# Binding the eight 64-column products of a pair of heads into one uninterrupted run on TensorE

## The chip, the cores and the metric

The kernel runs on one core of a Trainium2 chip. The metric is the device time of one execution in microseconds; the median of several runs is compared. Engines are called PE or TensorE (matrix products), PEld (its weight loads), DVE or VectorE, ACT or ScalarE, POOL or GpSimd, and SP (which issues most transfers).

## The reference, cut to what matters

The program is an encoder trunk of two layers on 512 tokens of 1024 features: feed-forward, token mixer, attention into a memory of 256 tokens, feed-forward, each followed by a layer norm. The change lies in the mixer of the first ("even") layer:

```python
def mixer_ab(h, w_in, w_out, q_gain, k_gain, sink, ang_2d, ang_1d):
    qa, ka, va, qb, kb, vb = jnp.split(h @ w_in, AB_SPLITS, axis=-1)
    ...                                   # per-head RMS norm of qa, ka; rotary of all q, k
    out_a = global_gqa(qa, ka, va)        # 8 query heads of 64, 2 key heads: every token sees every token
    out_b = window_gqa_sink(qb, kb, vb, sink)   # 8 heads: only tokens within +-128, a sink logit per head
    return jnp.concatenate([out_a, out_b], axis=-1) @ w_out

# for one head, in both halves:
    s = einsum('qd,sd->qs', q, k) * 64 ** -0.5
    p = softmax(s)
    o = einsum('qs,sd->qd', p, v)         # the product that the change concerns
```

## The kernel before

All 512 tokens stay on the chip. A matrix product of full precision is made of three products of rounded parts (`mm3`), in 512-column banks of PSUM; a bank is named by its tag: `a` (3 banks), `d` (2) and `t` (3). Sixteen heads are worked off in order, eight global ones (`weights_a`) and eight windowed ones (`weights_b`), two to a pair: pair `pr`, half `s`. For one head the steps are:

- `scores`: for each of four blocks of 128 queries two products into a bank `a` (512 columns; 256 or 384 for windowed heads).
- The minimum on VectorE, the exponential and the normalisation on ScalarE (`softmax`), into a tile `t2`.
- `turned`: for each block `kk` of 128 keys, TensorE transposes the weights into a bank `t` and a copy brings them to a `slab` tile; three copies run on VectorE, the one for `kk == 3` on ScalarE.
- `attend`, once for a pair: eight products into one bank `d`. Each multiplies 64 columns of values by the turned weights. The first head (`s == 0`) writes partitions 0 to 63 of the bank, the second 64 to 127, and the loop takes the heads alternately: block 0 of head 0, block 0 of head 1, block 1 of head 0, and so on. Both operands are plain float32, so that the profile has two records for each of these products ("128*64" in its rows; other products are "128*128").

Between the heads stands work of other kinds (`aside`): the last columns of the input projection (`last_columns`, 48 products a block into a bank `d`), the turning of the windowed values and keys, and shares of the output projection (`share`, 12 products of 512 columns into a bank `d`). After the mixer the memory stage follows, whose weights are loaded and split in two parts by ScalarE and VectorE while the mixer still runs.

None of this is the order in which instructions are issued. `Graph.record` writes every operation down with its dependences and a cost, so that all of them carry one line number in the profile (L159). `Graph.plan` then simulates the five engines with these costs and gives each engine a fixed order: whenever an engine is free, it takes the ready operation with the lowest key, the key being the place in the recorded program (`rank`), and for VectorE, ScalarE and GpSimd, in a second pass, the latest start that keeps TensorE on time (`deadlines`). If the product with the lowest key is not ready, another one goes first. For a product with 64 rows or columns the cost is halved (`beside` in `cost`).

Of the kernel before, what the change touches and what calls it, by code (L numbers as in the profile page):

```python
# [23 lines left out]
NT = S // P  # L24
# [41 lines left out]
class Graph:  # L66
# [3 lines left out]

    LATENCY = {"tensor": 200.0, "vector": 115.0, "scalar": 135.0, "gpsimd": 90.0, "sync": 90.0}
    PATIENT = ("vector", "scalar")
    URGENT = ("vector", "scalar", "gpsimd")
    ENGINES = ("tensor", "vector", "scalar", "gpsimd", "sync")

# [64 lines left out]
    def record(self, engine, method, args, kw):  # L140
        kw = dict(kw)
        aps = [z for z in list(args) + list(kw.values()) if hasattr(z, "tensor")]
        outs = [kw[k] for k in ("out", "accum_out") if k in kw]
        if "out" not in kw:
            outs.insert(0, args[0])
        ins = [z for z in aps if not any(z is o for o in outs)]
        op = Op()
        op.engine, op.index, op.dma, op.adds = engine, len(self.ops), method == "dma_start", "accum_op" in kw
        op.rank = op.index
        op.ns = self.cost(engine, method, outs[0], ins, kw)  # L150
        func = args[2] if method == "activation" else None
        op.table = str(func) if func in (AF.Silu, AF.Exp) else None
        op.size = math.prod(outs[0].shape) * 4
        op.thin = op.dma and engine == "sync" and op.size >= 2**19 and outs[0].shape[0] <= 64
        op.port = method in ("tensor_tensor", "scalar_tensor_tensor", "tensor_scalar") and (
            engine == "gpsimd" or engine == "vector" and math.prod(outs[0].shape[1:]) >= 64 and all(z.space != bass.MemoryType.PSUM for z in ins)
        )
        fn = getattr(getattr(self.nc, engine), method)
        op.call = lambda: fn(*args, **kw)  # L159
        op.deps, op.users, op.frees, op.later = set(), [], [], []  # L160
        if self.after and engine in self.after[1]:
            op.deps.add(self.after[0])
        for z, writes in [(z, False) for z in ins] + [(z, True) for z in outs]:
            info = self.tiles.get(z.tensor.name)
            if info is None:
                continue
            p0, p1, runs = self.extent(z)
            opens = writes and kw.get("start", False)
            keep = []
            for q, w, a0, a1, other in info["log"]:  # L170
                over = opens or p0 < a1 and a0 < p1 and (
                    info["bank"] and q.engine != engine or any(l < b and a < h for l, h in runs for a, b in other)
                )
                if over and (w or writes or info["bank"] and q.engine != engine) and q is not op:
                    op.deps.add(q)
                covered = writes and p0 <= a0 and a1 <= p1 and all(any(l <= a and b <= h for l, h in runs) for a, b in other)
                if not covered:
                    keep.append((q, w, a0, a1, other))
            keep.append((op, writes, p0, p1, runs))
            info["log"] = keep  # L180
            info["users"].add(op)
        self.ops.append(op)

    def plan(self):

# [28 lines left out]
        def arrive(e):  # L214
            while heaps[e] and heaps[e][0][0] <= now[e]:
                _, key, i, op = heapq.heappop(heaps[e])
                heapq.heappush(ready[e], (key, i, op))
# [6 lines left out]
        while len(order) < len(self.ops):  # L224
            best = None
            for e in self.ENGINES:
                arrive(e)
                if ready[e] and e in self.PATIENT:
                    key, _, op = ready[e][0]
# [72 lines left out]
    def emit(self):  # L302
# [10 lines left out]
        for op in self.ops:  # L313
            if op.engine in self.URGENT:
                op.key = last[op]
# [7 lines left out]
class Kernel:  # L323
# [683 lines left out]
    def mixer_ab(self, ln_i, last):  # L1007
        nc, a = self.nc, self.a
# [148 lines left out]
        def attend(po, pts, vp):  # L1157
            for kk in range(NT):
                for s in range(2):
                    lo, hi, pt = pts[s][kk]  # L1160
                    nc.tensor.matmul(
                        po[64 * s : 64 * s + 64, lo:hi], vp[:, kk, 64 * s : 64 * s + 64], pt, start=kk == 0, stop=kk == NT - 1,
                        skip_group_check=True,
                    )

        w2 = self.w_cols512(w_in, 1024)
        vt, vt_, qb_ = self.t2(F32), [], {}
# [42 lines left out]
        for n, (f, v, pr, s) in enumerate(heads):  # L1210
            pts = turned(us.pop(0))
            for g, _, *at in heads[n + 2 : n + 3]:
                us.append(g(*at))
            if s == 1 and n + 3 < len(heads):
                made[n >= 5, heads[n + 3][2]] = queries(qb if n >= 5 else qa, heads[n + 3][2], n >= 5)
            if s == 0:
                kept = pts
            else:
                po = self.ps("d")
                attend(po, (kept, pts), v if n < 8 else vb[0])  # L1220
                if n < 8:
                    acts.append(self.split_t2(po))
                else:

                    h, l = self.pair()
                    self.split(
                        po.rearrange("p (r c) -> p c r", r=ROWS), *(z.rearrange("p (c r) -> p c r", r=ROWS) for z in (h, l))
                    )
                    acts.append((h, l))
            for g in aside.get(n, []):  # L1230
                g()
            if n == 13:
                self.memory_tokens()
# [436 lines left out]
```

## Time and profile before

| | |
|---|---|
| median of 3 runs | 2127.72 us (2126.93 to 2129.83) |
| the profiled execution | 2127.48 us, of which the span of instructions 2125.7 us |
| granted TensorE clock | 0.998 of full speed |
| PE busy | 2109.5 us, 99% of the span |
| DVE busy | 1727.3 us, 81% |
| ACT busy | 1141.2 us, 54% |

Times in the views are counted from the start of the span. "Busy" is the time in which at least one instruction of the engine runs; products overlap their neighbours at both ends, so that the distance from one start to the next is the better price. In rows of the timeline, equal instructions that follow each other are one row with their count ("x3"), and a bracket at the end holds the idle time ahead of it and what ended that. The chain is followed back from the last instruction, from each step to what released it.

### The profile page before, as it was taken

How to read it: one execution, taken by the hardware profiler on the slowest of the kernel's cores; microseconds unless marked ns; L12 is line 12 of the kernel's file. 1: busy time of each engine (PE TensorE's matmuls, PEld its weight loads, DVE VectorE, ACT ScalarE, POOL GpSimd, SP SyncE). 2: the span in 40 equal slices, each digit the busy share in tenths (PEclk: the TensorE clock that was granted, in tenths of full speed). 3: DMA queues.
4: the chain of work that ended last, by engine and by line, in shares of the span. 5: the costliest groups of instructions: out<-in, count | busy, mean ns of one | idle time of the engine just before them, and what ended most of it. 6: DMA issues, size and time to landing. Idle time of an engine off the chain costs nothing.

```text
span 2125.7 us, 32517 instructions
## 1 busy us (share of the span) xinstructions
PE 2109.5 (99%) x12584; PEld 1850.5 (87%) x12584; DVE 1727.3 (81%) x2479; ACT 1141.2 (54%) x1855; POOL 278.4 (13%) x375
## 2 busy tenths in 40 slices
PE   9999999999999999999999999999999999999997
PEld 7999987767888899998889999888888888999996
DVE  7789988777748879998879999866578479699997
ACT  5555543687546554445445455457765465444552
POOL 0001014310002000000200000312210011000003
PEclk9999999999999999999999999999999999999999
DMA  6566562004433346664446556256454433456551
GB/s 205 142 167 148 135 189 90 21 21 119 138 121 109 90 123 175 153 156 129 149 100 147 123 138 190 73 143 168 118 164 156 139 91 98 109 149 154 144 150 60
DMA packets 208858, 275.91 MB, mean 130 GB/s; under 512 B 10688, under 2 KB 151616, under 8 KB 208704
## 3 DMA queue, kind: packets, MB, share of 16 engines
q1 hardware_dynamic: 175904, 221.14, 33.8%
q0 software_dynamic: 32512, 52.44, 14.2%
q8 instruction: 99, 1.62, 0.3%
q14 instruction: 55, 0.45, 0.1%
q10 hardware_dynamic: 288, 0.26, 0.0%
HBM read 259.12 MB, written 4.19 MB: 124 GB/s over the span
## 4 chain that ended last, share of the span: by engine, by line
PE 96%; DVE 2%; DMA 1%; ACT 1%; SPq 0%; issue 0%; DVEq 0%; POOL 0%; ACTq 0%
PE a L159 59%; PE d L159 23%; PE t L159 15%; DVE slab L159 1%; DVE x L159 1%; DMA slab<-t 1%; SPq L159 0%; ACT t L159 0%; DMA raw<-x_t 0%; ACT slab L159 0%; DVE t L159 0%; DVE xl L159 0%; ACT xh L159 0%; POOL lny L159 0%; DVEq L1666 0%
## 5 line engine op out<-in xcount | busy, mean ns | idle before, releaser
L159 DVE TENSOR_TENSOR slab<-slab,slab 128x1024 fp32r<-128x1024 f32 (+3 forms) x638 | 727.9, 1166 | 71.1 <-ACT slab L159 41.5
L159 ACT CAST slab<-slab 128x1024 fp32r<-128x1024 f32 (+2 forms) x498 | 472.4, 983 | 342.3 <-DVE slab L159 170.5
L159 PE MATMUL a<-slab,slab 128*128 128x256 f32 (+3 forms) x2320 | 566.7, 322 | 0.7 <-DMA slab<-t 0.5
L159 PE MATMUL a<-xh,slab 128*128 128x256 f32 (+2 forms) x2480 | 560.1, 315 | 0.1
L159 PEld LDWEIGHTS a<-slab,slab 128*128 128x128 f32 x2320 | 409.7, 190 | 45.6 <-ACT t L159 3.4
L159 PEld LDWEIGHTS a<-xh,slab 128*128 128x128 f32 x2480 | 416.5, 190 | 33.6 <-ACT slab L159 1.0
L159 PE MATMUL d<-slab,slab 128*128 128x512 f32 (+3 forms) x1792 | 442.5, 395 | 0.2 <-DVE x L159 0.2
L159 PE MATMUL a<-xl,slab 128*128 128x256 f32 (+1 forms) x1240 | 389.7, 314 | 0.0
L159 PE MATMUL a<-raw,slab 128*128 128x256 f32 x2048 | 389.0, 283 | 0.1
L159 PEld LDWEIGHTS d<-slab,slab 128*128 128x128 f32 (+1 forms) x1792 | 308.0, 185 | 66.8 <-issue 11.8
L159 PEld LDWEIGHTS a<-raw,slab 128*128 128x128 f32 x2048 | 327.9, 192 | 5.5 <-ACT slab L159 0.6
L159 PEld LDWEIGHTS a<-xl,slab 128*128 128x128 f32 x1240 | 236.1, 190 | 18.1
L159 PE MATMUL t<-slab,slab 128*128 128x512 f32 (+1 forms) x840 | 209.7, 389 | 1.0 <-DVE x L159 1.0
L159 DVE TENSOR_TENSOR slab<-raw,slab 128x1024 fp32r<-128x1024 f32 (+2 forms) x140 | 160.0, 1159 | 17.5 <-ACT slab L159 17.2
L159 PEld LDWEIGHTS t<-slab,slab 128*128 128x128 f32 x840 | 149.9, 189 | 27.5 <-issue 1.3
L159 ACT CAST slab<-raw 128x1024 fp32r<-128x1024 f32 (+1 forms) x132 | 124.2, 970 | 23.5 <-PE a L159 8.7
L159 DVE SCALAR_TENSOR_TENSOR x<-d,x 128x512 f32<-128x512 f32 x168 | 114.7, 685 | 23.5 <-PE d L159 22.6
L159 ACT COPY t<-a 128x512 f32<-128x512 f32 (+1 forms) x116 | 63.4, 549 | 129.9 <-PE a L159 76.7
L159 DVE TENSOR_TENSOR slab<-t,slab 128x512 fp32r<-128x512 f32 (+1 forms) x158 | 101.9, 660 | 12.8 <-ACT slab L159 12.5
L159 ACT CAST slab<-t 128x512 fp32r<-128x512 f32 (+1 forms) x158 | 90.2, 588 | 37.9 <-DVE t L159 14.4
L159 POOL DMA_DIRECT2D slab<-ffn_w_down x40 | 47.7, 1193 | 309.9 <-DVE slab L159 280.1
L159 ACT ACTIVATE t<-a 128x512 f32<-128x512 f32 (+3 forms) x65 | 36.3, 559 | 93.2 <-PE a L159 93.2
(127 smaller groups left out, 2191.3 us busy)
## 6 DMA issues: line engine op xcount, KB each, us to landing
slab<-ffn_w_gate SPq DMA_DIRECT2D x80, 512.0 KB
slab<-ffn_w_up SPq DMA_DIRECT2D x80, 512.0 KB
slab<-ffn_w_down SPq DMA_DIRECT2D x80, 512.0 KB
slab<-ffn_w_down POOLq DMA_DIRECT2D x40, 512.0 KB, 5.7
raw<-mem_w_kv SPq DMA_DIRECT2D x16, 1024.0 KB
slab<-t SPq DMA_DIRECT2D x96, 128.0 KB
slab<-ffn_w_gate POOLq DMA_DIRECT2D x16, 512.0 KB, 7.6
slab<-ffn_w_up POOLq DMA_DIRECT2D x16, 512.0 KB, 6.0
```

Source lines behind the costliest of these rows:

```text
L159: op.call = lambda: fn(*args, **kw)
```

## The change

After the eight products of a pair are recorded, `join` binds them. The first product gets the dependences of all eight, so the planner lets the run begin only when everything that it reads is there. Each of the others depends on the one before it and gets the rank -1, which makes it the first choice of TensorE as soon as its predecessor is issued. The planner's cost of the first and of the last product rises by 95 ns each. Only the planned order changes; what an instruction on the chip waits for is still its own operands.

```diff
     PATIENT = ("vector", "scalar")
+    TURN = 95.0
     URGENT = ("vector", "scalar", "gpsimd")
...
+    def join(self, n):
+
+        run = self.ops[-n:]
+        for prev, op in zip(run, run[1:]):
+            run[0].deps |= op.deps.difference(run)
+            op.deps.add(prev)
+            op.rank = -1
+        run[0].ns += self.TURN
+        run[-1].ns += self.TURN
...
                         skip_group_check=True,
                     )
+            nc.join(2 * NT)
```

The built programs hold the same instructions. Three places of TensorE's order follow. In the names, `d_725`, `d_893` and `d_942` are the banks of the first, fourth and fifth pair; `slab_556` and `slab_754` hold values of global and windowed heads; the other `slab` of a 64-row product holds turned weights; `ident` marks a transpose.

TensorE at the first pair, from its first product on, before (`slab_676`, `slab_679` are the turned weights of head 0, `slab_702`, `slab_705` those of head 1; `a_693` to `a_715` are scores of a later head):

```order
L159 MATMUL d_725_806<-slab_676_757,slab_556_637 64x512
L159 MATMUL a_693_774<-slab_600_681,slab_668_749 128x512 x2
L159 MATMUL a_707_788<-slab_602_683,slab_668_749 128x512
L159 MATMUL t_706_787<-ident_1_78,t2_653_734 128x128
L159 MATMUL t_706_787<-ident_1_78,t2_657_738 128x128
L159 MATMUL t_706_787<-ident_1_78,t2_661_742 128x128
L159 MATMUL t_706_787<-ident_1_78,t2_665_746 128x128
L159 MATMUL a_707_788<-slab_602_683,slab_668_749 128x512
L159 MATMUL a_711_792<-slab_602_683,slab_668_749 128x512 x2
L159 MATMUL d_725_806<-slab_702_783,slab_556_637 64x512
L159 MATMUL a_715_796<-slab_602_683,slab_668_749 128x512 x2
```

Two products stand alone; after the last row and four transposes come a piece of two, two scores and a piece of four. The same place now:

```order
L160 MATMUL d_725_806<-slab_676_757,slab_556_637 64x512
L160 MATMUL d_725_806<-slab_702_783,slab_556_637 64x512
L160 MATMUL d_725_806<-slab_676_757,slab_556_637 64x512
L160 MATMUL d_725_806<-slab_702_783,slab_556_637 64x512
L160 MATMUL d_725_806<-slab_679_760,slab_556_637 64x512
L160 MATMUL d_725_806<-slab_705_786,slab_556_637 64x512
L160 MATMUL d_725_806<-slab_679_760,slab_556_637 64x512
L160 MATMUL d_725_806<-slab_705_786,slab_556_637 64x512
L160 MATMUL a_719_800<-slab_602_683,slab_668_749 128x512 x2
```

The scores `a_693` to `a_715` and the transposes `t_706` moved ahead of the run, which is unbroken and takes the heads in turn.

TensorE at the fourth pair, where the windowed heads begin, before (`t_895` are the first transposes of a windowed head, `slab_850` and `slab_873` the turned weights of key blocks 2 and 3 of the two heads; two more products of this pair stand alone further up):

```order
L159 MATMUL d_893_974<-slab_870_951,slab_556_637 64x512 x2
L159 MATMUL d_893_974<-slab_850_931,slab_556_637 64x512
L159 MATMUL d_893_974<-slab_873_954,slab_556_637 64x512
L159 MATMUL d_893_974<-slab_850_931,slab_556_637 64x512
L159 MATMUL d_893_974<-slab_873_954,slab_556_637 64x512
L159 MATMUL t_895_976<-ident_1_78,t2_853_934 128x128
L159 MATMUL t_895_976<-ident_1_78,t2_857_938 128x128
```

And now (`d_917` is a share of the output projection):

```order
L160 MATMUL t_895_976<-ident_1_78,t2_853_934 128x128
L160 MATMUL d_917_998<-slab_813_894,slab_839_920 128x512
L160 MATMUL t_895_976<-ident_1_78,t2_857_938 128x128
L160 MATMUL a_887_968<-slab_845_926,slab_837_918 128x256 x2
L160 MATMUL d_917_998<-slab_812_893,slab_839_920 128x512
L160 MATMUL d_893_974<-slab_847_928,slab_556_637 64x512
L160 MATMUL d_893_974<-slab_870_951,slab_556_637 64x512
L160 MATMUL d_893_974<-slab_847_928,slab_556_637 64x512
L160 MATMUL d_893_974<-slab_870_951,slab_556_637 64x512
L160 MATMUL d_893_974<-slab_850_931,slab_556_637 64x512
L160 MATMUL d_893_974<-slab_873_954,slab_556_637 64x512
```

The transposes `t_895` now stand ahead of the fourth pair's run, and seven products of the share stand ahead of them, where three did before.

TensorE at the fifth pair, before (its first three products, two of 256 and 384 columns together and one of 384, stand a few rows further up; `t_940` turns queries, `a_936` are scores):

```order
L159 MATMUL d_942_1023<-slab_899_980,slab_754_835 64x256
L159 MATMUL d_944_1025<-slab_809_890,slab_726_807 128x512
L159 MATMUL t_923_1004<-ident_1_78,t2_884_965 128x128
L159 MATMUL t_923_1004<-ident_1_78,t2_888_969 128x128
L159 MATMUL d_942_1023<-slab_919_1000,slab_754_835 64x256
L159 MATMUL t_940_1021<-ident_1_78,slab_554_635 128x128
L159 MATMUL t_940_1021<-ident_1_78,slab_555_636 128x128 x2
L159 MATMUL t_940_1021<-ident_1_78,slab_556_637 128x128
L159 MATMUL d_942_1023<-slab_919_1000,slab_754_835 64x384
L159 MATMUL d_942_1023<-slab_922_1003,slab_754_835 64x384
L159 MATMUL a_936_1017<-slab_845_926,slab_892_973 128x256 x2
L159 MATMUL d_942_1023<-slab_922_1003,slab_754_835 64x256
```

And now:

```order
L160 MATMUL d_942_1023<-slab_896_977,slab_754_835 64x256
L160 MATMUL d_942_1023<-slab_919_1000,slab_754_835 64x256
L160 MATMUL d_942_1023<-slab_896_977,slab_754_835 64x384
L160 MATMUL d_942_1023<-slab_919_1000,slab_754_835 64x384
L160 MATMUL d_942_1023<-slab_899_980,slab_754_835 64x384
L160 MATMUL d_942_1023<-slab_922_1003,slab_754_835 64x384
L160 MATMUL d_942_1023<-slab_899_980,slab_754_835 64x256
L160 MATMUL d_942_1023<-slab_922_1003,slab_754_835 64x256
L160 MATMUL a_936_1017<-slab_845_926,slab_892_973 128x256 x2
```

Six pieces became one run; of the share `d_944`, one product stood ahead of the last piece before, and four stand ahead of the run now.

## The prediction

> **What bounds the kernel now.** I read the page's first part, then the chain that ended last, then the waits of TensorE in the mixer (390 to 560 us), to see whether time taken from TensorE there is time taken from the end.
>
> ```profile
> PE 2109.5 (99%) x12584; PEld 1850.5 (87%) x12584; DVE 1727.3 (81%) x2479; ACT 1141.2 (54%) x1855; POOL 278.4 (13%) x375
> ...
> PE 96%; DVE 2%; DMA 1%; ACT 1%; SPq 0%; issue 0%; DVEq 0%; POOL 0%; ACTq 0%
> ...
> PE d L159 <- DVE x L159: 0.2, 1, 0.2
> ```
>
> TensorE holds 96% of the chain, and the last row is the only recorded wait in those 170 us (columns: us in total, times, longest). So the end moves with TensorE's own time, until another engine becomes late. A busy TensorE is not one at its peak, though, so next I asked what the 64-column products cost. Each of the eight pairs of heads has a bank `d` of its own; this view takes TensorE's work on `d` in eight stretches, one for each pair (columns: stretch, its length, busy us and records).
>
> ```profile
> 409.50:418.23 8.73, 5.09 (x16) 1.00 0.00 0
> 431.00:436.35 5.35, 4.64 (x16) 1.00 0.00 0
> 449.20:453.68 4.48, 3.79 (x16) 1.00 0.10 24
> 458.10:468.60 10.50, 5.72 (x16) 1.00 0.09 28
> 473.90:482.66 8.76, 5.98 (x18) 1.00 0.00 0
> 493.85:496.19 2.34, 2.29 (x16) 1.00 0.05 3
> 506.20:509.50 3.30, 2.93 (x16) 1.00 0.73 278
> 517.20:521.08 3.88, 3.58 (x16) 1.00 0.19 36
> sum 47.34, PE 34.02; mean PE 4.25
> ```
>
> The work is equal in the first four (global heads, 512 columns) and equal in the last four (windowed heads, 256 or 384), and every product is two records, yet the cost goes from 3.79 to 5.72 and from 2.29 to 5.98. The timeline of the first pair tells why (start, us, then what ran; the distance to the next row is what a row really takes).
>
> ```profile
> 409.57 1.07 PE L159 MATMUL d<-slab,slab 128*64 128x512 f32 x2
> 410.57 0.96 PE L159 MATMUL a<-slab,slab 128*128 128x512 f32 x3
> ...
> 414.70 1.08 PE L159 MATMUL d<-slab,slab 128*64 128x512 f32 x4
> 415.71 0.73 PE L159 MATMUL a<-slab,slab 128*128 128x512 f32 x2
> 416.37 1.94 PE L159 MATMUL d<-slab,slab 128*64 128x512 f32 x8
> 418.24 0.72 PE L159 MATMUL d<-slab,xh 128*128 128x512 f32 x2
> ```
>
> One product alone (x2) takes 1.00 us, two products (x4) take 1.01, four take 1.87. The two heads of a pair use different halves of the array's columns and run side by side if they stand next to each other; a lone one leaves half of the array empty for a whole microsecond. A further pair in a run costs 1.87 - 1.01 = 0.86.
>
> **The change, part by part.** It adds no instruction and removes none. The built orders differ on TensorE between the transposes of the first pair and the mixer's last rows, on VectorE and ScalarE in the same stretch, and in a swap of two output transfers at the very end, of the same size and not the last to leave, which I cost at nothing. The transfers on POOL keep their order, and SP's keep theirs but for that swap; so SP's loads of weights are moved past nothing. All eight pairs stand as unbroken runs of eight, heads alternating, where before there were 22 pieces (4, 2, 2, 3, 6, 1, 2, 2 by pair).
>
> *Term 1, the products themselves.* The price of a bound run is in the trace: for windowed heads the sixth stretch, 2.29; for global heads 1.01 + 3 x 0.86 = 3.59, and the same from a piece of seven products that fills four places:
>
> ```profile
> 432.78 3.65 PE L159 MATMUL d<-slab,slab 128*64 128x512 f32 x14
> 436.36 0.73 PE L159 MATMUL d<-slab,xh 128*128 128x512 f32 x2
> ```
>
> That is 3.58. Eight runs: 4 x 3.58 + 4 x 2.29 = 23.48, against 34.02, a difference of 10.54. Two corrections: the fifth stretch holds two 128-column products of another `d` (x18), about 0.5; and the busy time of each piece runs 0.07 into the next row (409.57 + 1.07 against 410.57), which 14 pieces fewer no longer do: 1.0. Term 1 is **-9.0 us**.
>
> *Term 2, the turns.* Work between two pieces is itself slower. The third pair shows two score products squeezed between two halves, and an earlier row shows six in one go:
>
> ```profile
> 449.29 1.94 PE L159 MATMUL d<-slab,slab 128*64 128x512 f32 x8
> 451.16 0.74 PE L159 MATMUL a<-slab,slab 128*128 128x512 f32 x2
> 451.82 1.94 PE L159 MATMUL d<-slab,slab 128*64 128x512 f32 x8
> 453.69 0.66 PE L159 MATMUL t<-ident,t 128*128 128x128 f32 x4
> ...
> 406.46 1.54 PE L159 MATMUL a<-slab,slab 128*128 128x512 f32 x6
> 407.84 0.40 PE L159 MATMUL d<-slab,xl 128*128 128x512 f32 x1
> ```
>
> Two squeezed products take 451.82 - 451.16 = 0.66; at the free pace (1.38 / 6 = 0.23) they take 0.46. So a break costs 0.20 outside the pieces, beside what term 1 holds. 14 breaks go: **-2.8 us**. [...] Were the turn free, the sum would rest on term 1 alone, 2.8 us higher.
>
> *Term 3, what is late next.* A lone product used to be issued as soon as its own operand was there; now it stands behind work that was pulled ahead of it, and TensorE reaches that work sooner. What must keep up is VectorE and ScalarE. Their load from the first piece to the last, and in two stretches where the present kernel runs them hard (columns: stretch, length, then busy us of PE, PEld, DVE, ACT, POOL):
>
> ```profile
> 409.60:521.00 111.40, 111.16 (x587) 75.40 (x586) 87.93 (x243) 91.01 (x217) 10.45 (x40) 1.00 0.18 48
> 490.00:510.00 20.00, 20.00 (x121) 15.28 (x120) 18.36 (x55) 17.80 (x47) 2.25 (x8) 1.00 0.58 159
> 535.00:560.00 25.00, 25.00 (x133) 21.25 (x132) 23.80 (x38) 14.20 (x22) 2.22 (x6) 1.00 0.37 118
> ```
>
> 111.40 less 11.8 is 99.6: VectorE would be busy for 88% of it and ScalarE for 91%. The other two rows have them at 92% and 89%, and at 95% and 57%, with no wait on TensorE. So the load is bearable; queues are the danger. The tightest place that I find is the passage to the windowed heads, where the first transposes of a windowed head (`t_895`) now stand ahead of the fourth pair's run instead of behind it. Before, it reads:
>
> ```profile
> 447.16 0.60 PE L159 MATMUL t<-ident,t 128*128 128x128 f32 x4
> ...
> 468.61 0.76 PE L159 MATMUL t<-ident,t 128*128 128x128 f32 x5
> ...
> 448.27 0.58 ACT L159 COPY slab<-t 128x512 f32<-128x512 f32 x1
> ...
> 449.40 0.59 ACT L159 ACTIVATE slab<-t 64x512 fp32r<-64x512 f32 x1 [0.55 <-PE t L159]
> ...
> 453.81 0.59 ACT L159 CAST slab<-d 128x512 fp32r<-128x512 f32 x1 [1.05 <-PE d L159]
> ...
> 459.89 0.58 ACT L159 COPY slab<-t 128x512 f32<-128x512 f32 x1 [0.78 <-PE t L159]
> ...
> 464.10 0.59 ACT L159 COPY slab<-t 128x512 f32<-128x512 f32 x1 [0.83 <-PE t L159]
> ...
> 465.09 1.91 ACT L159 ACTIVATE t<-t,l 128x256 f32<-128x256 f32 x4
> ```
>
> From the transposes that feed the 448.27 copy to `t_895`, TensorE took 468.61 - 447.16 = 21.45. Now the three pieces of the fourth pair (1.00 + 1.00 + 3.58) and four breaks (0.8) leave that stretch, two score products of 256 columns follow instead of preceding (0.2), the third pair's halves shrink by 0.15, and four more products of the output share, seven for three, come in (0.9): about 15.6. ScalarE, from that copy to the normalisation at 465.09, took 16.82, of which the four idle times are 3.21: 13.6 of work. The margin was 468.61 - 465.09 - 0.50 = 3.0 and is now 15.6 - 13.6, or 2.0 less whatever idling ScalarE keeps. Should it keep all 3.2, TensorE waits 1.2. The same squeeze in the fifth pair, whose stretch loses 5.98 to 2.29 and already held the 0.2 wait, I put at 0.8. So **+2.0 us**; the ends are -1.0 (no wait at all, and the short stalls on transposes there shrink too) and +7 (the squeeze at each of six later pairs).
>
> *Inside a run* I cost waiting at nothing: the copy that comes last, of the other head's third and fourth key block, is read first by the sixth product, 5 x 0.43 = 2.1 us after a global run's start, which is the cover. If the copy is later than that, TensorE stands still with the rest of its queue.
>
> Sum: 2127.48 (the profiled execution: span 2125.7 and 1.8 around it; 0.24 below the median shown) - 9.0 - 2.8 + 2.0 = **2117.7 us**.
>
> **The rivals.** (A) *The softmax chain keeps its pace.* Scores, minimum, exponential, normalisation, transposes and copies run round over ScalarE, and what TensorE saves it waits. [...] Against: its idle times are mostly waits for TensorE (`PE t`, `PE d` in the rows above), which shrink with it. If waits take back 10 of the 11.8 us the time is 2125.7: no change. (B) *The next stage is not ready.* The memory projections start 12 us sooner, and their weights pass through VectorE:
>
> ```profile
> 553.33 1.21 DVE L159 TENSOR_TENSOR slab<-raw,slab 128x1024 fp32r<-128x1024 f32 x1
> ...
> 557.41 1.07 PE L159 MATMUL a<-slab,slab 128*128 128x512 f32 x4
> ```
>
> This half is done at 554.54 and first read within the second row, 3.2 us later. If VectorE's queue, 95% full there, did not move at all, TensorE would wait 11.8 - 3.2 = 8.6, and 2124.3 results. Against: the split stands between parts of the layer norm that are released by TensorE, and so it moves with it. (C) *Slower:* each run waits for its last copy, because ScalarE has exponentials ahead of it, and nothing else may pass. With w us for each of eight runs the gain is gone at w = 11.8 / 8 = 1.5 and the kernel is slower beyond the bound at w = 2.0; at 2.5 it takes 2135.7. Against it stands the 2.1 us of cover, so that a copy would have to be over 4 us late, eight times, where the whole stretch now has one wait. (D) *Nothing is saved:* the runs are unbroken but some of them do not overlap their halves, as in the piece at 465.03 before, where two products of one head stood together. The new order alternates throughout, so I hardly believe it.
>
> **How the numbers follow.** The forecast has 0.76, and its own range is 2127.5 - 11.8 - 1.0 = 2114.7 to 2127.5 - 11.8 + 7 = 2122.7. (A) has 0.09, (B) 0.09, (C) 0.04, (D) 0.02. About 0.2% (4.3 us) is what a measurement here can tell from no change; faster means below 2123.5. The forecast is faster wholly, of (A) and (B) together 0.05, when waits take back only part. So faster 0.81, same 0.15, slower 0.04. The range of 0.8 runs from 2114.0 to 2123.5: the likeliest case whole, and its edge of (A) and (B).
>
> **What would show it.** In the profile after, stretches of `d` should read about 3.6 and 2.3 with x16 each, their sum near 23.5 (terms 1 and 2 right); score products beside a run should keep the 0.66 only once for each side. Waits of TensorE on `a`, `t` or `d` within the mixer should add up to about 2 us; if they add up to 8 or more, (A) or (C), told apart by whether a `t`/`a` row or a `d` row waits; waits on `a` at the start of the memory stage mean (B). Rows from the memory stage on should be the old ones shifted by some 10 us. I am wrong if ScalarE's order puts copies behind exponentials that themselves wait, which no trace of the old order can show.

## The result, and the profile after

| | before | after |
|---|---|---|
| median | 2128.38 us (4 runs, one more than above) | 2115.42 us (2114.70 to 2117.81, 4 runs) |
| ratio | | 0.9941 (95% interval 0.9924 to 0.9958) |
| ratio of a second measurement (5 runs, 2115.9 us) | | 0.9947 (0.9935 to 0.9960) |
| profiled execution, span | 2127.48, 2125.7 us | 2117.81, 2116.0 us; second one: span 2113.8 us |

The kernel is faster by 0.5 to 0.6%, 12 to 13 us. The page's first part and its chain after the change:

```profile
PE 2099.0 (99%) x12584; PEld 1847.6 (87%) x12584; DVE 1725.2 (82%) x2479; ACT 1141.1 (54%) x1855; POOL 280.3 (13%) x375
...
PE 95%; DVE 2%; DMA 1%; ACT 1%; SPq 1%; issue 0%; DVEq 0%; POOL 0%; ACTq 0%
```

The counts are the old ones, and PE is busy for 10.5 us less. TensorE's work on `d` in the eight stretches, one for each pair, as it was shown of before (columns: stretch, its length, busy us and records, then granted clock and DMA; in four rows the product ahead of the run ends just inside the stretch, hence x17):

```profile
413.40:417.05 3.65, 3.57 (x16) 1.00 0.00 0
430.40:434.06 3.66, 3.57 (x16) 1.00 0.00 0
447.50:451.10 3.60, 3.58 (x16) 1.00 0.00 0
462.27:465.86 3.59, 3.59 (x17) 1.00 0.02 5
472.45:474.75 2.30, 2.30 (x17) 1.00 0.00 0
484.60:486.94 2.34, 2.29 (x16) 1.00 0.00 0
497.97:500.27 2.30, 2.30 (x17) 1.00 0.42 169
509.65:511.95 2.30, 2.30 (x17) 1.00 1.06 370
sum 23.74, PE 23.50; mean PE 2.94
```

All global pairs cost the same, all windowed ones too, and each at the price of the best unbroken run of before (3.58 and 2.30 from start to next start): 23.50 against 34.02. Where the mixer ends, at the memory stage's first key products, TensorE stands here, before and after (timelines of the two kernels; start, us, what ran):

```profile
548.10 1.19 PE L159 MATMUL a<-slab,slab 128*128 128x512 f32 x5
```

```profile
536.94 1.41 PE L160 MATMUL a<-slab,slab 128*128 128x512 f32 x6
```

The first changed instruction starts at 408.49 before and 408.91 after, so that the mixer holds nearly the whole gain and the memory stage starts without delay. For every kernel below I give the same measure: the distance from the first changed transpose to the first product behind the last changed row, 139.61 us before and 128.35 after ("the mixer"), and in it the sum of the pieces, from each piece's start to the next start ("the pieces", 32.66 and 23.55). The rest is 106.95 and 104.80.

### The profile page after: what moved, and what is told of

Same layout as the page of the kernel before. It is cut to its first block, busy times and chain, and to the rows that moved or that the text cites. A ratio compares the mean times of both kernels' runs of the same rounds, so it can differ in the third digit from the quotient of the medians.

```text
span 2116.0 us, 32513 instructions
## 1 busy us (share of the span) xinstructions
PE 2099.0 (99%) x12584; PEld 1847.6 (87%) x12584; DVE 1725.2 (82%) x2479; ACT 1141.1 (54%) x1855; POOL 280.3 (13%) x375
## 4 chain that ended last, share of the span: by engine, by line
PE 95%; DVE 2%; DMA 1%; ACT 1%; SPq 1%; issue 0%; DVEq 0%; POOL 0%; ACTq 0%
PE a L160 59%; PE d L160 22%; PE t L160 14%; DMA slab<-t 1%; DVE slab L160 1%; ACT t L160 1%; SPq L160 1%; DVE x L160 1%; DMA raw<-c_w_out 0%; DVE t L160 0%; ACT slab L160 0%; DMA raw<-x_t 0%; DVE xl L160 0%; ACT xh L160 0%; DVE mn L160 0%
## 5 line engine op out<-in xcount | busy, mean ns | idle before, releaser
L160 PE MATMUL d<-slab,slab 128*128 128x512 f32 (+4 forms) x1792 | 432.0, 394 | 0.0
```

## The experiments

| kernel | median, ratio to before (interval) | pieces | mixer |
|---|---|---|---|
| changed kernel again | 2115.90, 0.9947 (0.9935 to 0.9960) | 23.55 | 128.34 |
| bound in twos | 2119.74, 0.9960 (0.9948 to 0.9973) | 24.46 | 130.81 |
| head by head | 2128.45, 1.0002 (0.9993 to 1.0011) | 35.13 | 139.83 |
| two and two | 2117.19, 0.9951 (0.9936 to 0.9966) | 23.96 | 128.67 |
| windowed pairs only | 2122.28, 0.9976 (0.9967 to 0.9985) | 28.00 | 134.16 |
| global pairs only | 2120.90, 0.9966 (0.9953 to 0.9978) | 27.63 | 132.95 |
| no extra planner cost | 2119.62, 0.9962 (0.9949 to 0.9976) | 23.55 | 129.97 |
| larger extra planner cost | 2119.14, 0.9959 (0.9947 to 0.9972) | 23.55 | 130.57 |
| dependences not gathered | 2123.37, 0.9978 (0.9968 to 0.9987) | 27.87 | 134.29 |
| more work on ScalarE | 2119.28, 0.9958 (0.9945 to 0.9972) | 23.55 | 130.11 |

**The changed kernel again**, without an edit.

> The changed kernel once more, for a tighter ratio and a second profile. In the first profile the mixer stretch of TensorE, from the first changed transpose to the first row after the last changed one, lasts 128.35 us (139.61 before), and 2.4 us of waits for the small transfers slab<-t stand in the odd mixer (0.5 before). If these waits belong to one execution alone, this profile has the same 128.3 us in the even mixer and about 0.5 us in the odd one; if they are a lasting price of the new order, about 2.4 again. Time 2115 to 2117 us, ratio near 0.994.

The mixer is the same to 0.01 us. The waits for the small transfers `slab<-t` in the odd mixer, of before, of the first and of the second profile after (us in total, times, longest):

```profile
PE a L159 <- DMA slab<-t: 0.5, 2, 0.3
```

```profile
PE a L160 <- DMA slab<-t: 2.4, 6, 0.5
```

```profile
PE a L160 <- DMA slab<-t: 0.7, 3, 0.3
```

The same kernel shows 2.4 and 0.7, so most of the 2.4 belonged to that execution and not to the order; the first profile caught the slowest of its four runs.

**Head by head or two by two.** Is it the overlap of the two halves that pays, or the unbroken run?

```diff
-            for kk in range(NT):
-                for s in range(2):
+            for s in range(2):
+                for kk in range(NT):
```

> Eight products of a pair still bound in one run, but the four of the first head first and then the four of the second, so that neighbours use the same half of the columns. Theory 1: only the fourth and fifth product of a run can overlap; 7 places of 0.86 us instead of 4 in a global run, and the like in a windowed one: the runs add up to about 40.8 us instead of 23.55, the mixer to about 145.6, the time to about 2132.6, slower than the kernel before by 0.2%. Theory 2 (turns and the unbroken run alone): the same number of runs, so the mixer stays near 128.4 and the time near 2115.4.

The eight runs stand unbroken, and the whole gain is gone: the time is that of before (1.0002, interval 0.9993 to 1.0011). The first run (timeline; the next row's start ends it):

```profile
413.03 5.42 PE L160 MATMUL d<-slab,slab 128*64 128x512 f32 x16
418.38 0.72 PE L160 MATMUL a<-slab,slab 128*128 128x512 f32 x2
```

It takes 418.38 - 413.03 = 5.35 instead of 3.58. What lies outside the pieces keeps its gain (139.83 - 35.13 = 104.70, against 104.80 in the changed kernel and 106.95 before), so fewer breaks are worth some 2.2 us by themselves; the pieces lose 11.6 us with the overlap and are 2.5 longer than before, which eats it up. So unbroken runs paid here only because their halves overlap (3.58 us against 5.35). My size was wrong, though: seven places of 0.86 were counted and six were taken, so the pieces add up to 35.13 and not 40.8, and the kernel is no slower than before where 0.2% was expected. Why six? In the second variant the order is 0, 0, 1, 1, 0, 0, 1, 1 by heads.

```diff
-            for kk in range(NT):
-                for s in range(2):
-                    lo, hi, pt = pts[s][kk]
+            for s, kk in [(s, kk) for half in range(2) for s in range(2) for kk in (2 * half, 2 * half + 1)]:
+                for lo, hi, pt in (pts[s][kk],):
```

> The eight products of a pair bound in the order two of the first head, two of the second, two of the first, two of the second. Taking heads one by one (four and four) a global run took 5.35 us, six places of 0.86 and the turns, where I had counted seven. Theory A (TensorE starts a product of the free half up to two products, four records, ahead of its turn): two and two overlap wholly, a global run takes 3.6 us and a windowed one 2.3, the time is that of the bound kernel, 2115 to 2117. Theory B (products start in the order of the program, and the six places had another cause): five to six places, a global run takes 4.4 to 5.2 us, the eight runs 28 to 33 us, and the time is 2120 to 2125.

```profile
413.14 3.71 PE L160 MATMUL d<-slab,slab 128*64 128x512 f32 x16
416.77 0.74 PE L160 MATMUL a<-slab,slab 128*128 128x512 f32 x2
```

3.63 us: all but the 3.58 of the alternating order. Theory A's forecast of 3.6 us holds; the starts of the records stand at the end.

**Bound in twos**, so that no product is alone but work may come between.

```diff
-            nc.join(2 * NT)
+                nc.join(2)
```

> Only the two products of one key block, one of each head, are bound; other work may stand between such twos. The built order has 14 pieces (8 in the bound kernel, 22 before), and no product alone. Theory 1 (a lone product leaves half of the array empty, and beside that each break costs about 0.35 us, 0.15 of it inside the piece and 0.2 outside): the pieces add up to about 24.5 us (23.55 bound, 32.66 before), the mixer to about 130.4 us, the time to about 2117.5. Theory 2 (it is the unbroken run of eight as such that saves): 6 of the 14 saved breaks are back, so 6/14 of the 11.3 us saved are lost: mixer 133.2, time about 2120.

The first pair shows a break:

```profile
411.88 1.08 PE L160 MATMUL d<-slab,slab 128*64 128x512 f32 x4
412.89 0.73 PE L160 MATMUL a<-slab,slab 128*128 128x512 f32 x2
...
414.45 2.80 PE L160 MATMUL d<-slab,slab 128*64 128x512 f32 x12
417.17 0.50 PE L160 MATMUL d<-slab,xh 128*128 128x512 f32 x1
```

1.01 and 2.72 are 3.73 where an unbroken run takes 3.58: a break costs 0.15 inside. Six more breaks made the pieces 24.46 - 23.55 = 0.91 longer (0.15 each, as theory 1 had it), and the rest of the mixer 106.35 - 104.80 = 1.55, of which about 0.6 are short stalls that were added (records that take over 0.05 us more than others between the same neighbours) and 0.16 a break are left. The mixer, 130.8, is that of theory 1 (130.4), not of theory 2 (133.2); the median, 2119.7, is nearer to theory 2's. What it has beyond the mixer lies outside; two places there differ between executions and kernels (below), but that they make it up is not shown.

**Half of the pairs.** First the windowed ones alone, then the global ones alone.

```diff
-            nc.join(2 * NT)
+            if vp is not va:
+                nc.join(2 * NT)
```

> Only the four windowed pairs are bound; the four global ones are planned as before. The built order has 15 pieces: 11 global ones, with the same split as before the change, and 4 runs. Theory 1: the pieces add up to 28.1 us (-4.5 against before), seven breaks fewer take another 0.16 each outside (-1.1): mixer about 134.0 us, time about 2122. Rival (the gain comes from the shorter softmax chain at the passage to the windowed heads, where the fourth pair now stands behind the first windowed transposes): with the fourth pair split as before, most of the windowed gain is lost again in waits and the mixer stays above 137 us.

Pieces 28.00 (28.1 expected), mixer 134.16 (134.0), median 2122.3 (2122): theory 1 to within 0.2 us. The rival, by which the gain lies at the passage to the windowed heads, had the mixer above 137.

```diff
-            nc.join(2 * NT)
+            if vp is va:
+                nc.join(2 * NT)
```

> The complement of the windowed experiment: only the four global pairs are bound. The built order has 14 pieces: 4 runs and ten windowed pieces, split much as before the change. Theory 1 (lone products and breaks): the pieces add up to 27.7 us (-4.9 against before) and eight breaks fewer take 0.16 each outside (-1.3): mixer about 133.4 us, time about 2121.5; with the -5.44 us that binding the windowed pairs alone gave, the two halves add up to the -11.26 us of the whole change. Theory 3 (the parts help each other, by what is pulled forward): the sum of the halves falls short of the whole by 2 us or more, so that this mixer stays above 135 us.

Pieces 27.63 (27.7 expected), mixer 132.95 (133.4), median 2120.9. The halves save 5.45 and 6.66, together 12.1, where the whole change saves 11.26. Theory 3 wanted the halves to save 2 us or more less than the whole; they save 0.85 more, so it fails. Of the 0.85, 0.58 lies in the pieces: with only the global pairs bound, the windowed ones fell into ten pieces of 13.29 us, where before they were eleven of 13.87. The gain is, but for such bits, a sum over the pairs.

**How it is bound.** The run's first product no longer gets the dependences of the others:

```diff
-            run[0].deps |= op.deps.difference(run)
```

> join without the line that gives the first product the dependences of all eight: a run may begin when its first operand is there, and if a later one is not, other work is put between. The built order has 17 pieces, five of them begin with a product alone and four end with one. Theory 1: the pieces add up to 28.0 us (+4.4 against the bound kernel) and nine more breaks take 0.16 each (+1.4): mixer about 134.2 us, time about 2121.5. Rival (TensorE waits inside the runs, so that the line's worth is the waits it avoids): the pieces stay as long as in theory 1, but waits on d of 2 us or more come on top.

Pieces 27.87 (28.0 expected), mixer 134.29 (134.2). The waits of TensorE in the mixer:

```profile
PE t L160 <- ACT t L160: 0.9, 1, 0.9
PE t L160 <- DVE slab L160: 0.3, 1, 0.3
```

None is on `d`: no run waits inside; the run just falls apart, since a product whose operand is late lets other work in. The line matters for 5.9 us of the mixer, half of the gain there. The median, 2 us above the expectation, is not explained by the mixer. Then the planner's cost of the turn, 0 and 180 instead of 95:

```diff
-    TURN = 95.0
+    TURN = 0.0
```

> The runs stay bound, and the planner's extra 95 ns for the first and the last product are set to 0. Theory 1: the order has the same 8 runs (23.55 us) and the planner is 0.2 us a run more hopeful, which moves few rows: mixer within 1 us of 128.35, time within 2 us of the bound kernel. Rival (the planner's knowledge of the turn is what keeps TensorE from waiting): the mixer gets 2 us or more longer, with recorded waits on t or d.

```diff
-    TURN = 95.0
+    TURN = 180.0
```

> The bound kernel with 180 ns instead of 95 ns as the planner's extra cost of the first and the last product, since a break was measured at about 0.35 us. Theory (the planner's times only have to be roughly right): the same 8 runs, mixer within 0.7 us of 128.35, time 2115 to 2117. Rival (a truer cost lets TensorE wait less): the 1.3 us of short stalls that are left in the mixer shrink, mixer 127.3, time 2114.5.

The pieces stay, and both mixers are longer, by 1.6 and 2.2 us. Both theories missed: the first allowed 1 us and 0.7, the rival of the first wanted 2 us or more with waits on `t` or `d`, the rival of the second wanted it faster. The waits in the mixer with 180 are

```profile
PE t L160 <- DVE slab L160: 0.7, 1, 0.7
PE t L160 <- ACT t L160: 0.5, 1, 0.5
PE a L160 <- DVE mn L160: 0.3, 1, 0.3
```

and short stalls, as defined above, add up to about 3.4 us (3.0 with 0, 1.3 in the changed kernel). Neither a lower nor a truer cost helps, yet three points do not make 95 an optimum: small shifts of the planned order move the stalls by some 2 us.

**How near ScalarE is to being the limit.** Eight more copies, one for each global head:

```diff
                 self.softmax(u, P, mn, 0, S, sums=ps)
+                if t == 0:
+                    nc.scalar.activation(self.junk[:, :512], u, AF.Copy)
```

> The bound kernel with eight more copies on ScalarE, one of 128x512 for each global head, into a tile that nobody reads: some 8 x 0.7 = 5.6 us of ScalarE between 409 and 465 us, where ScalarE is busy for 51.5 of 56 us and TensorE has no recorded wait. If the idle rest of 4.5 us can be used, TensorE loses about 1 us (mixer 129.5, time 2117). If ScalarE's idle time is bound in the chain and can't be used, so that the softmax chain was already at its limit, TensorE loses nearly all of it (mixer 134, time 2121).

From 409 to 512 us, the changed kernel and this one (stretch, length, busy us of PE, PEld, DVE, ACT, POOL):

```profile
409.00:512.00 103.00, 103.00 (x605) 75.10 (x604) 89.49 (x248) 93.62 (x223) 11.24 (x41) 1.00 0.23 62
```

```profile
409.00:512.00 103.00, 102.14 (x595) 73.72 (x594) 88.96 (x247) 95.84 (x228) 11.26 (x41) 1.00 0.19 52
```

The copies took 0.64 us each, 5.1 in all, and the mixer grows by 1.76, a third of that, between the two expectations and nearer to the first. So ScalarE, at 91%, was not yet the limit. How much room is left is not shown: the copies also shift the planned order, and the two kernels above lost 1.6 and 2.2 us by such a shift alone. At 93% TensorE has holes of 0.86 us in this stretch, and the largest waits for VectorE (waits of TensorE in the mixer):

```profile
PE t L160 <- DVE slab L160: 0.7, 1, 0.7
PE a L160 <- ACT t L160: 0.2, 1, 0.2
```

## Why the prediction was right

Forecast 2117.7 us with a range of 2114.0 to 2123.5; measured 2115.4 and 2115.9. The direction and the mechanism of terms 1 and 2 hold, by the experiments and not only by the sum; term 3 does not.

- **Term 1, the products: -9.0 forecast, -9.1 measured** (32.66 to 23.55). That a lone product takes the time of two (1.00 us against 1.01 before) is what decides it: the order that keeps the runs and takes away the overlap loses all 11 us of the mixer.
- **Term 2, the turns: -2.8 forecast, -2.15 measured** for everything outside the pieces (106.95 to 104.80), what term 3 came to included; the two other orders of eight runs give 104.70 and 104.71. The order in twos gives 0.16 for a break outside the piece; I had taken 0.20 from a break with products on both sides. By the records of before, the row ahead of a piece takes 0.1 us longer; behind it a product takes 0.335 instead of 0.227 us, a transpose only 0.164 instead of 0.109, and some breaks had transposes behind them.
- **Term 3, the new waits: +2.0 forecast, about +0.1 measured.** This is the mis-sized step. No wait of TensorE is recorded in the mixer, not at the fifth pair either, and its short stalls went from about 1.2 to 1.3 us. The passage to the windowed heads, after the change:

```profile
445.34 0.66 PE L160 MATMUL t<-ident,t 128*128 128x128 f32 x4
...
461.27 0.27 PE L160 MATMUL t<-ident,t 128*128 128x128 f32 x1
...
446.08 0.57 ACT L160 COPY slab<-t 128x512 f32<-128x512 f32 x1
447.31 0.69 ACT L160 ACTIVATE t<-a,mn 128x512 f32<-128x512 f32 x1 [0.66 <-DVE mn L160]
...
451.25 0.59 ACT L160 CAST slab<-d 128x512 fp32r<-128x512 f32 x1 [0.50 <-PE d L160]
...
460.35 1.00 ACT L160 ACTIVATE t<-t,l 128x256 f32<-128x256 f32 x2
```

TensorE needs 461.27 - 445.34 = 15.93 (15.6 forecast). ScalarE idles 1.16 instead of 3.21 and is done with the first normalisation at 460.85: a margin of 0.42, where I had let it keep all its idling and had TensorE wait 1.2. All four of the old idle times waited for TensorE; 0.50 us of that is left, and 0.66 now waits for VectorE.

The margin itself was also worked out wrongly. In the 3.0 of before, the 1.11 us from the transposes to the copy (448.27 - 447.16) and the 0.50 of the first normalisation are taken off; in the new 15.6 - 13.6 = 2.0 they are not. Worked out alike it is 0.4 with no idling, and with all of it TensorE would have waited 2.8. So the 1.2 holds two errors that stand against each other. Against that 0.4, ScalarE kept 1.16 of idling, but it had 13.1 us of work instead of 13.6, its copy followed the transposes by 0.74 instead of 1.11, and TensorE took 0.3 longer: 0.42. That no wait came at all was a near thing.

That the place is tight is right all the same: the kernels with an extra cost of 0 and 180 and the one with more work on ScalarE lose 1.6 to 2.2 us in the mixer, and 1.9 to 2.4 us of their short stalls stand between 453 and 473 us, around this passage, against 0.2 in the changed kernel.

- **(A), the chain keeps its pace:** did not happen. ScalarE's load rose to 91% as worked out, and the added copies show that most of 5.1 us more of its work still found room.
- **(B), the next stage is not ready:** did not happen; the memory stage's rows are the old ones 11 us earlier.
- **(C), runs wait for their last copy:** no run does, in any of the kernels. The cover was a little less than the 2.1 us that I gave: products run in twos, so the fifth and sixth start together, 415.25 - 413.48 = 1.77 us after the first run's start.
- **(D), runs that do not overlap:** not in this order; the head-by-head kernel shows what it would have been.

Not foreseen at all is a place in the odd layer, which the change does not touch. A split on VectorE beside additions on POOL (before, then the second profile after; VectorE, then POOL):

```profile
1359.92 3.64 DVE L159 TENSOR_TENSOR slab<-slab,slab 128x1024 fp32r<-128x1024 f32 x1
...
1357.42 5.05 POOL L159 TENSOR_TENSOR x<-x,slab 128x512 f32<-128x512 f32 x4
1364.24 3.00 POOL L159 TENSOR_TENSOR x<-x,slab 128x512 f32<-128x512 f32 x2 [1.77 <-DVE x L159]
```

```profile
1349.15 2.40 DVE L160 TENSOR_TENSOR slab<-slab,slab 128x1024 fp32r<-128x1024 f32 x1
...
1346.65 9.01 POOL L160 TENSOR_TENSOR x<-x,slab 128x512 f32<-128x512 f32 x6
```

The same split takes 3.64 or 2.40 us (the difference, 1.24, is about the length of one of the additions, 5.05 / 4), and TensorE behind it is held up by 1.1 us more or less. It is 3.64 before and in the profiles of head by head, two and two, windowed only and more ScalarE work, and 2.40 in the others. So about 1 us of the 12 between the profiles is not the mixer's, and whether it comes with the new timing or by chance is open. This and the transfers of the odd mixer may be why the medians of these kernels lie up to 2 us further from the changed kernel's than their mixers do; only profiled executions can be looked into, so it is not shown.

## What to carry to other kernels

Products that use half of the array's columns were cheap only in company here (1.00 us for one of 512 columns alone, 1.01 for two of different halves): look in the timeline for pieces of one product, price them from the start of the next row, and count how often they occur before believing that TensorE at 99% has no slack. A planner that halves their cost regardless of the neighbour does not see this. Binding them into one run mended it here, when the run alternated between the halves closely enough (3.58 us in turn, 3.63 two and two, against 5.35 head by head) and began only when the operands of all were there; without the latter, half of the gain was lost. Before charging waits to the engine behind TensorE, subtract that part of its idling which is itself waiting for TensorE, and count the same steps in the margin before and after.

## What the runs showed of the hardware

By the starts of the records, products of the second head started ahead of their turn in these runs. With four products of one head before four of the other, the second head's first record starts 0.006 us after the first head's fifth of eight, so the second head begins in the third place instead of the fourth, and the run takes six places (5.35 us) instead of seven. With two and two, the two heads' first records start 0.014 us apart, and the run takes 3.63 us against 3.58 in turn. In both runs the record that started early stands four records, two products, further on in the order than the one beside which it started. The records do not name the half, so this rests on times alone. Had every product waited for its turn (theory B), two and two would have taken five places or more, by estimate 4.3 us at 0.86 a place; the measured 3.63 us does not agree, and the measurement decides.
